# Gated DeltaNet and sliding-window decoder trunk on one core: the mixer's last four gated heads kept in rows, the key halves exchanged by DMA, and other first and last steps of the attention

## The chip, the core and the metric

The kernel runs on one core of a Trainium2 chip. Its time is the device time of one execution in microseconds (us); the time of a version is the median over its runs. The engines are PE (TensorE: matmuls and transposes through the identity), PEld (the weight loads of TensorE, which lie beside the matmuls), DVE (VectorE), ACT (ScalarE), POOL (GpSimd) and SP (SyncE, which here only issues transfers). "L821" is line 821 of the kernel before; where a line of the changed kernel is meant, it says so.

## The reference

The input is x, 512 tokens of 1024 features, in float32. Two layers follow one another:

```python
h = x
h = h + gated_deltanet(rmsnorm(h), w_in, conv_w, ..., w_out)    # layer 0: token mixer
h = h + conv_gated_mlp(rmsnorm(h), w_up, conv_w, conv_b, w_down)
k, v = shared_kv(h, kv_norm_w, w_kv)                            # 4 key and value heads of 64
h = h + sliding_window_sink_attention(rmsnorm(h), k, v, w_q, ..., w_o)   # 16 query heads, window 128
h = h + conv_gated_mlp(rmsnorm(h), ...)
return rmsnorm(h, final_norm_w)
```

Two pieces matter here. The mixer has 16 value heads of 128; at its end each head's output o is normalised and gated, and all heads are projected:

```python
o = rmsnorm(o, out_norm_w) * jax.nn.silu(z)
return o.reshape(bsz, t, GDN_V_DIM) @ w_out
```

The attention has four query heads to a key head: p = softmax over 256 keys and a sink of (q k / 8 + bias), masked to the window; the output p v goes through w_o.

## The kernel before

**Numbers as pairs.** A float32 matrix product is made of three matmuls for each 128 rows of depth: both factors are split into a high part that the matmul takes exactly and the rest (hi and lo), and `mm3` (L158) issues hi by hi (L162), hi by lo (L163) and lo by hi (L164). `split` (L167) makes such a pair of a row of 128 x 512: a cast on ACT (L168) gives hi, a subtraction on DVE (L169) gives lo. Weights come in stages of 1024 x 256 (`load_stage`, L120, two buffers) and are split by `cast` (a cast on ACT, L132, and a subtraction on DVE, L133) into the three buffers each of `whi` and `wlo`.

**Buffers.** Activations lie in rows of 128 x 512 float32, each under a name (`va`, `us`, `p6s`, `dt`, `sz`, `zl`) with a few buffers that go round. A name gives its next buffer out when the last reader of that buffer is done. PSUM has eight banks: three called d, two g, two s, one p.

**End of the mixer.** The table ORDER and the priorities SHIFT set the order of the mixer's jobs: projections, the recurrent `scan` (L609) over four chunks, the gate. `gate_proj` (L684) projects the gate z of a head and writes silu(z) to DRAM (`zd`, L689); `scan` writes o to DRAM (`od`, L666). `gate(h)` (L692) loads o of head h into `dt` (L696) and z into `va` (L697), scales o by its norm on ACT (four instructions of 128 x 128, L700), transposes it on PE into a g bank (L703), multiplies with z on DVE in place (L704) and writes the row to DRAM (`yd`, L705). The last four heads (12 to 15) come after the last chunk of the scan; for them `va` has two buffers. The out-projection then loads each head's row from `yd` (L801) into the rows called "u" (`sz`, `sz`, `zl`), splits it, and multiplies by w_out (`mm3`, the weights from `a_w_out`). Beside it x itself is loaded (L818), transposed on PE into g banks (L821) and copied to the residual rows by ACT (L822); the loads for the last two of its eight parts use buffers that the first two must have left.

**Start of the attention** (`attention`, L1140). Keys and values are projected from the normalised residual. Each of the two key rows holds two key heads of 64. Scores take 64 partitions of queries against 64 partitions of keys, so each key head is needed in both halves of the partitions: L1164 to L1167 cast and subtract every half row twice, into its own half (`near`) and into the other (`far`), eight casts of 64 x 512 on ACT and eight subtractions on DVE. Values are transposed on PE (L1171) and copied by ACT. Then the queries are projected pair by pair (`query`, matmuls L1181, L1183, L1185), and each of the 16 half pairs goes through `scores` (L1224, with a reduction on DVE, L1232, an exponential on ACT, L1249, and a scaling on DVE, L1253), `turn_back` (transposes of the probabilities, L1260) and `values` (L1276). On PE this stretch is in an order that is written out: a generator `dense` gives the matmuls of the later queries and of the first five depth steps of three output tiles one by one, and `take` puts 11 or 12 of them after each half pair.

**End of the attention.** After the last half pair come `values(14)`, the rest of the generator, `turn_back(15)`, depth steps 5 and 6 of the three open output tiles (`late_outputs`), `values(15)`, depth step 7 tile by tile with the addition to the residual on DVE (L1311), and the other five output tiles.

Of the kernel before, what the change touches and what calls it, by code (L numbers as in the profile page):

```python
# [12 lines left out]
ALU = mybir.AluOpType  # L13
# [28 lines left out]
def kernel(  # L42
# [164 lines left out]
    def columns(parts, n, s, q=SP, tag="acc"):  # L207
# [6 lines left out]
        ps = bank("g")  # L214
# [476 lines left out]

    def gate(h):  # L692
        ot, y = (row("ol"), row("zl")) if h < 12 else (row("dt"), row("va"))
# [11 lines left out]
        SP.dma_start(yd[h], y[:])  # L705
# [434 lines left out]
    def attention(h):  # L1140
        toep = rb[:]

        keys = [wide("G") for g in range(4)]
        kxh, kxl = normed(h, NKV)
        for kv in range(2):
# [10 lines left out]
            for i, ps in enumerate(products):  # L1156
                f = r2("va")
                V.tensor_tensor(f[:], ps[:], rs[:], op=ALU.mult)
                if kv == 0:
                    for j in range(2):  # L1160
                        g = 2 * i + j
                        near, far = [slice(64 * u, 64 * u + 64) for u in (j, 1 - j)]
                        src, hi = f[near, :], keys[g][near, 0, :]
                        S.copy(hi, src)  # L1164
                        S.copy(keys[g][far, 0, :], src)
                        V.tensor_tensor(keys[g][near, 1, :], src, hi.bitcast(F32), op=ALU.subtract)
                        V.tensor_tensor(keys[g][far, 1, :], src, hi.bitcast(F32), op=ALU.subtract)  # L1167
                else:
                    pt = bank("g")
                    for c in range(NC):  # L1170
                        PE.transpose(pt[:, c * P : (c + 1) * P], f[:, c * P : (c + 1) * P], ident[:])  # L1171
# [6 lines left out]

        def one_by_one(ps, w, k, xh, xl, first, last):
            hi, lo = w  # L1180
            PE.matmul(ps, hi[:, k, :], xh, start=first, stop=False)  # L1181
# [28 lines left out]
        def scores(u):  # L1210
            p, n0 = u // 2, 2 * (u % 2)
            (qh, ql), b3 = queries[p], bias[p]
            kh, kl = [keys[p // 2][:, i, :] for i in range(2)]
# [4 lines left out]
            for n in (n0, n0 + 1):  # L1218
# [3 lines left out]
                for i, (q, k) in enumerate(((qh, kh), (qh, kl), (ql, kh))):  # L1222
                    for j, hs in enumerate(half):
                        PE.matmul(sc[j][:, at], q[hs, ns], k[hs, k0 : k0 + W], start=i == 0, stop=i == 2)  # L1224
# [82 lines left out]
        def late_outputs(opened, k):  # L1307
            for m, (ps, w) in enumerate(opened):
                yield from one_by_one(ps[:], w, k, ah[k], al[k], False, k == KD - 1)
# [99 lines left out]
```

## Time and profile before

| | |
|---|---|
| median of 3 runs | 1426.94 us (1426.77 to 1426.95) |
| the profiled execution's own time | 1428.72 us |
| its span, from first to last instruction | 1426.9 us |
| mean granted TensorE clock | 0.998 |
| PE busy | 1389.5 us, 97% of the span |
| DVE, ACT, POOL busy | 1113.8, 753.8 and 13.0 us |
| moved by DMA | 152.85 MB, 107 GB/s on average |

The profile is a trace of one execution. A row of a timeline has the start in us from the span's start, the length in us, the engine, the line, the operation, what it writes and reads, a count where several were joined, and in brackets how long the engine had been idle and what ended that. A row of the waits has the engine, what waited, who released it, and the time that was waited. In the windows a row has the stretch, its length, then the busy time and the count of PE, PEld, DVE, ACT and POOL, the granted clock of PE as a share of full speed, the busy share of the DMA engines and GB/s. Matmuls overlap: a row's length is longer than the pace at which they follow one another, so stretches are priced by the distance between starts.

### The profile page before, as it was taken

What the parts mean: (1) busy time and instruction counts of PE and PEld (TensorE: products, weight loads), DVE (VectorE), ACT (ScalarE), POOL (GpSimd) and SP (SyncE); (2) the same over time, 40 slices, a digit from 0 to 9 for tenths busy, and PEclk for the clock granted to TensorE, in tenths of its full rate; (3) what the DMA queues carried; (4) which work ended last, traced back from release to release, by engine and by line L of the source; (5) the groups of instructions that cost most, each with busy time, mean ns of one, the idle gap of its engine ahead of it and who ended that gap; (6) DMA issues with size and microseconds to landing.
All of it is one profiled execution on the core that took longest, in us unless ns stands there. A gap on an engine that the chain in (4) does not pass through costs nothing.

```text
span 1426.9 us, 21762 instructions
## 1 busy us (share of the span) xinstructions
PE 1389.5 (97%) x8362; PEld 1165.5 (82%) x8362; DVE 1113.8 (78%) x2078; ACT 753.8 (53%) x1475; POOL 13.0 (1%) x37
## 2 busy tenths in 40 slices
PE   7999999999998999999999999999999999999997
PEld 5777878878876888888988889778788888988897
DVE  4996887969854447889878889878568888878996
ACT  7764566666546434444334446667544544344443
POOL 1000000000000000000000000000000000000000
PEclk9999999999999999999999999999999999999999
DMA  5324254264466324221443223122132322332222
GB/s 159 103 63 142 79 175 122 73 187 127 141 204 213 118 64 140 90 89 45 133 148 117 75 77 110 55 93 75 38 122 78 111 81 68 125 112 88 96 75 74
DMA packets 163131, 152.85 MB, mean 107 GB/s; under 512 B 24212, under 2 KB 150741, under 8 KB 163029
## 3 DMA queue, kind: packets, MB, share of 16 engines
q1 hardware_dynamic: 160770, 151.27, 33.0%
q8 instruction: 66, 1.08, 0.3%
q10 hardware_dynamic: 2259, 0.20, 0.1%
q14 instruction: 36, 0.29, 0.1%
HBM read 134.65 MB, written 16.80 MB: 106 GB/s over the span
## 4 chain that ended last, share of the span: by engine, by line
PE 82%; DVE 8%; DMA 6%; ACT 2%; issue 1%; DVEq 0%; SPq 0%; ACTq 0%
PE d L162 19%; PE d L163 19%; PE d L164 19%; DVE wlo L133 2%; PE s L617 1%; PE d L1030 1%; PE d L1185 1%; PE d L1028 1%; PE d L1183 1%; PE d L1181 1%; PE d L1029 1%; PE g L1260 1%; PE s L1030 1%; PE p L1276 1%; PE s L657 1%
## 5 line engine op out<-in xcount | busy, mean ns | idle before, releaser
L162 PE MATMUL d<-xh,whi 128*128 128x512 f32 x1128 | 445.1, 396 | 0.2
L163 PE MATMUL d<-xl,whi 128*128 128x512 f32 x1128 | 444.0, 395 | 0.0
L164 PE MATMUL d<-xh,wlo 128*128 128x512 f32 x1128 | 443.2, 395 | 0.7 <-DVE wlo L133 0.4
L132 ACT CAST whi<-stage 128x1024 fp32r<-128x1024 f32 (+2 forms) x234 | 227.3, 975 | 229.2 <-PE d L163 146.8
L133 DVE TENSOR_TENSOR wlo<-stage,whi 128x1024 fp32r<-128x1024 f32 (+2 forms) x234 | 263.5, 1129 | 66.7 <-ACT whi L132 66.2
L164 PEld LDWEIGHTS d<-xh,wlo 128*128 128x128 f32 x1128 | 211.6, 188 | 45.6 <-DVE wlo L133 1.1
L162 PEld LDWEIGHTS d<-xh,whi 128*128 128x128 f32 x1128 | 211.7, 188 | 44.1 <-ACT xh L172 0.5
L163 PEld LDWEIGHTS d<-xl,whi 128*128 128x128 f32 x1128 | 211.7, 188 | 42.9 <-issue 0.5
L260 DVE SCALAR_TENSOR_TENSOR acc<-d,cwc,acc 128x511 f32<-128x511 f32 (+2 forms) x96 | 70.7, 738 | 12.2 <-ACT acc L257 11.6
L911 ACT ACTIVATE dt<-dt 128x512 f32<-128x512 f32 x44 | 27.8, 632 | 80.1 <-DVE dt L894 80.1
L889 DVE TENSOR_TENSOR sz<-d,p6s 128x512 f32<-128x512 f32 x58 | 40.0, 689 | 36.9 <-PE d L164 35.0
L894 DVE SCALAR_TENSOR_TENSOR va<-sz,fcw,va 128x511 f32<-128x511 f32 (+1 forms) x58 | 43.4, 748 | 1.7 <-ACT va L892 0.9
L894 DVE SCALAR_TENSOR_TENSOR dt<-sz,fcw,dt 128x511 f32<-128x511 f32 (+1 forms) x58 | 43.4, 748 | 0.9
L546 DVE TENSOR_TENSOR sT<-sT,p6s 64x31 f32<-64x31 f32 (+15 forms) x124 | 40.8, 329 | 2.2 <-DVE p6s L540 0.3
L540 DVE TENSOR_TENSOR p6s<-sN,sT 64x31 f32<-64x31 f32 (+15 forms) x124 | 40.5, 327 | 2.4 <-DMA sN<-nd 0.4
L1249 ACT ACTIVATE dt<-dt,sm 128x256 f32<-128x256 f32 (+1 forms) x64 | 30.1, 471 | 19.2 <-DVE sm L1232 19.1
L132 ACT CAST whi<-st 128x768 fp32r<-128x768 f32 (+1 forms) x30 | 23.7, 792 | 30.1 <-PE p L1029 5.8
L889 DVE TENSOR_TENSOR zl<-d,p6s 128x512 f32<-128x512 f32 x30 | 20.7, 689 | 24.0 <-PE d L164 23.7
L665 ACT ACTIVATE rq<-o 128x128 f32<-128x128 f32 x64 | 19.0, 298 | 28.6 <-DVE o L660 16.0
L913 DVE TENSOR_TENSOR va<-dt,va 128x512 f32<-128x512 f32 x44 | 30.4, 691 | 1.2
L133 DVE TENSOR_TENSOR wlo<-st,whi 128x768 fp32r<-128x768 f32 (+1 forms) x30 | 26.9, 903 | 2.2 <-ACT whi L132 2.2
L892 ACT ACTIVATE dt<-sz,normc,fcw 128x512 f32<-128x512 f32 x29 | 23.6, 814 | 7.2 <-DVE sz L889 7.2
(770 smaller groups left out, 2866.7 us busy)
## 6 DMA issues: line engine op xcount, KB each, us to landing
stage<-in_ffn_w_up_dram SPq DMA_DIRECT2D x44, 1024.0 KB, 4.9
stage<-in_a_w_in_dram SPq DMA_DIRECT2D x23, 1024.0 KB, 5.1
stage<-in_ffn_w_down_dram SPq DMA_DIRECT2D x16, 768.0 KB, 6.1
stage<-in_a_w_out_dram SPq DMA_DIRECT2D x8, 1024.0 KB, 4.9
st<-in_ffn_w_down_dram SPq DMA_DIRECT2D x8, 768.0 KB
zd<-sz SPq DMA_DIRECT2D x16, 256.0 KB, 2.0
od<-o SPq DMA_DIRECT2D x16, 256.0 KB, 3.7
stage<-in_b_w_q_dram SPq DMA_DIRECT2D x4, 1024.0 KB
```

The source lines that it names most:

```text
L132: S.copy(hi[:, :kt, :m], src)
L133: V.tensor_tensor(lo[:, :kt, :m], src, hi[:, :kt, :m].bitcast(F32), op=ALU.subtract)
L162: PE.matmul(ps, hi[:, k, :m], xh[k], start=first and k == 0, stop=False)
L163: PE.matmul(ps, hi[:, k, :m], xl[k][:], start=False, stop=False)
L164: done.append(PE.matmul(ps, lo[:, k, :m], xh[k], start=False, stop=last and k == kt - 1))
L260: V.scalar_tensor_tensor(acc[:, d:], ps[:, : T - d], col, acc[:, d:], op0=ALU.mult, op1=ALU.add)
L540: V.tensor_tensor(tv, N[:, s, s + 1 : 32].unsqueeze(2).to_broadcast([64, n, m]), Tm[:, s : s + 1, 0:m].to_broadcast([64, n, m]), op=ALU.mult,)
L546: V.tensor_tensor(Tm[:, s + 1 : 32, 0:m], Tm[:, s + 1 : 32, 0:m], tv, op=ALU.subtract)
L889: V.tensor_tensor(u[:], ps[:], rs[:], op=ALU.mult)
L894: V.scalar_tensor_tensor(acc[:, d:], u[:, : T - d], tap(2 - d, t), acc[:, d:], op0=ALU.mult, op1=ALU.add)
L913: V.tensor_tensor(b[:], a[:], b[:], op=ALU.mult)
L1249: S.activation(ej, ej, AF.Exp, bias=ngm[:, i : i + 1], scale=-1.0, accum_out=den[:, i : i + 1])
```

## The change

Six edits, in three places of the kernel; line numbers here are those of the changed kernel.

- **Gate.** Heads 12 to 15 take their gated row in `va`, `va`, `us` and `p6s`, and keep it there; the write to `yd` and the load back are left out for them, and the projection splits straight from these rows.
- **Keys.** One cast and one subtraction of 128 x 512 split a key row for two heads at once; the halves are exchanged into a second pair by DMA, four transfers on SP's queue (L1174), and `scores` takes the head from whichever pair has it in the right half.
- **Table.** A one-column exponential of ACT stands ahead (L1182).
- **Values' transposes** may not be issued ahead of the fourth hi-by-hi matmul of the first query.
- **First half pairs.** Eight of the twelve dense matmuls after the second half pair stand ahead of `turn_back(0)` instead of behind it.
- **Last half pair.** The generator is drained first, nine of the late matmuls follow, then `turn_back(15)`, `values(14)`, five more, `values(15)`, the last four; depth step 7 goes through the three tiles hi by hi, lo by hi and hi by lo, and the three additions come with the last of these.

```diff
     def gate(h):
-        ot, y = (row("ol"), row("zl")) if h < 12 else (row("dt"), row("va"))
+        ot = row("ol" if h < 12 else "dt")
+        y = row("zl") if h < 12 else row(("va", "va", "us", "p6s")[h - 12])
...
-        SP.dma_start(yd[h], y[:])
+        if h < 12:
+            SP.dma_start(yd[h], y[:])
+        else:
+            gated[h] = y
...
-            yr = r2("u")
-            SP.dma_start(yr[:], yd[2 * h2 + j])
+            if h2 < 6:
+                yr = r2("u")
+                SP.dma_start(yr[:], yd[2 * h2 + j])
+            else:
+                yr = gated[2 * h2 + j]
             split(yr[:], a[:, j, :], b[:, j, :])
...
                 if kv == 0:
-                    for j in range(2):
-                        g = 2 * i + j
-                        near, far = [slice(64 * u, 64 * u + 64) for u in (j, 1 - j)]
-                        src, hi = f[near, :], keys[g][near, 0, :]
-                        S.copy(hi, src)
-                        S.copy(keys[g][far, 0, :], src)
-                        V.tensor_tensor(keys[g][near, 1, :], src, hi.bitcast(F32), op=ALU.subtract)
-                        V.tensor_tensor(keys[g][far, 1, :], src, hi.bitcast(F32), op=ALU.subtract)
+                    near, far = keys[i]
+                    split(f[:], near[:, 0, :], near[:, 1, :])
+                    for a, b in ((slice(0, 64), slice(64, 128)), (slice(64, 128), slice(0, 64))):
+                        SP.dma_start(far[a, :, :].bitcast(F32), near[b, :, :].bitcast(F32))
...
+        S.activation(warm[:], rs[:, 0:1], AF.Exp, scale=0.0)
...
+        for t in turned_values:
+            behind(t, issued[3])
...
+                if u == 1:
+                    take(stream, 8)
                 if u > 0:
                     turn_back(u - 1)
-                take(stream, 12 if u < 12 else 11)
-            values(14)
+                take(stream, 4 if u == 1 else 12 if u < 12 else 11)
             for _ in stream:
                 pass
+            rest = late_outputs(opened, range(begun, KD - 1))
+            take(rest, 9)
             turn_back(15)
-            for k in range(begun, KD - 1):
-                for _ in late_outputs(opened, k):
-                    pass
+            values(14)
+            take(rest, 5)
             values(15)
-            for _ in late_outputs(opened, KD - 1):
+            for _ in rest:
                 pass
+            for i in range(3):
+                for m, (ps, w) in enumerate(opened):
+                    PE.matmul(ps[:], w[i % 2][:, KD - 1, :], (ah, ah, al)[i][-1], start=False, stop=i == 2)
+                    if i == 2:
+                        V.tensor_tensor(hT[m], hT[m], ps[:], op=ALU.add)
```

A new argument `place` of `columns` has a default that is the old value and isn't used. What the three places look like in the order of the instructions:

SP's queue at the end of the mixer. `stage` is a weight stage, `f` the rows for x. Before:

```order
L801 DMA sz_4534<-yd 128x512
L122 DMA stage_4755<-in_a_w_out_dram 128x8x256
L705 DMA yd<-va_4325 128x512
L705 DMA yd<-va_4438 128x512
L697 DMA va_4453<-zd 128x512
L801 DMA sz_4544<-yd 128x512
L697 DMA va_4468<-zd 128x512
L801 DMA sz_4548<-yd 128x512
L705 DMA yd<-va_4453 128x512
L818 DMA f_4575<-in_x_dram 128x4x128
L705 DMA yd<-va_4468 128x512
L801 DMA zl_4554<-yd 128x512
```

The same place now, and ahead of it the loads of z for heads 15 and 14:

```order
L689 DMA zd<-sz_4433 128x512
L122 DMA stage_4741<-in_a_w_out_dram 128x8x256
L700 DMA p6s_4465<-zd 128x512
L666 DMA od<-o_4198 128x512
...
L700 DMA us_4451<-zd 128x512
L666 DMA od<-o_4278 128x512
...
L808 DMA zl_4534<-yd 128x512
L122 DMA stage_4743<-in_a_w_out_dram 128x8x256
L827 DMA f_4563<-in_x_dram 128x4x128
L827 DMA f_4564<-in_x_dram 128x4x128
```

The writes of four gated rows, the four loads back and the two loads of z that stood between them are gone from here; the loads of z for heads 14 and 15 are now further up, among the writes of the scan's chunks, and the loads of x follow the weight stage directly.

PE at `turn_back(0)`. `s` are the scores, `g` the banks of the transposes, `d` the dense matmuls. Before:

```order
L1224 MATMUL s_8787<-kT_8384,S_8691 128x256
L1224 MATMUL s_8788<-kT_8384,S_8691 128x256
L1260 MATMUL g_8820<-ident_81,dt_8736 128x128 x2
L1260 MATMUL g_8825<-ident_81,dt_8743 128x128 x4
L1181 MATMUL d_8770<-xh_8639,whi_8771 128x512
```

Now:

```order
L1236 MATMUL s_8768<-kT_8372,S_8672 128x256
L1236 MATMUL s_8769<-qT_8373,S_8672 128x256
L1192 MATMUL d_8751<-xh_8619,whi_8752 128x512
L1194 MATMUL d_8751<-xl_8620,whi_8752 128x512
L1196 MATMUL d_8751<-xh_8619,wlo_8753 128x512
L1192 MATMUL d_8751<-xh_8623,whi_8752 128x512
L1194 MATMUL d_8751<-xl_8624,whi_8752 128x512
L1196 MATMUL d_8751<-xh_8623,wlo_8753 128x512
L1192 MATMUL d_8751<-xh_8627,whi_8752 128x512
L1194 MATMUL d_8751<-xl_8628,whi_8752 128x512
L1272 MATMUL g_8809<-ident_81,dt_8717 128x128 x2
L1272 MATMUL g_8814<-ident_81,dt_8724 128x128 x4
```

Eight dense matmuls have come between the second scores and the transposes, and the two heads' scores read the keys from two tiles, `kT` and `qT`.

PE at the end of the attention, where `p` is the bank of the last values and the three banks d are the open output tiles. Before, from `values(15)` on:

```order
L1276 MATMUL p_9873<-acc_9893,Vp 64x128 x4
L1181 MATMUL d_9646<-at_9846,whi_9647 128x512
L1183 MATMUL d_9646<-at_9847,whi_9647 128x512
L1185 MATMUL d_9646<-at_9846,wlo_9648 128x512
L1181 MATMUL d_9721<-at_9846,whi_9722 128x512
L1183 MATMUL d_9721<-at_9847,whi_9722 128x512
L1185 MATMUL d_9721<-at_9846,wlo_9723 128x512
L1181 MATMUL d_9797<-at_9846,whi_9798 128x512
L1183 MATMUL d_9797<-at_9847,whi_9798 128x512
L1185 MATMUL d_9797<-at_9846,wlo_9799 128x512
L162 MATMUL d_9936<-sy_8964,whi_9937 128x512
```

Now, from the last of the four matmuls that stand behind `values(15)`:

```order
L1196 MATMUL d_9778<-at_9827,wlo_9780 128x512
L1365 MATMUL d_9627<-at_9827,whi_9628 128x512
L1365 MATMUL d_9702<-at_9827,whi_9703 128x512
L1365 MATMUL d_9778<-at_9827,whi_9779 128x512
L1365 MATMUL d_9627<-at_9827,wlo_9629 128x512
L1365 MATMUL d_9702<-at_9827,wlo_9704 128x512
L1365 MATMUL d_9778<-at_9827,wlo_9780 128x512
L1365 MATMUL d_9627<-at_9828,whi_9628 128x512
L1365 MATMUL d_9702<-at_9828,whi_9703 128x512
L1365 MATMUL d_9778<-at_9828,whi_9779 128x512
L162 MATMUL d_9917<-sy_8945,whi_9918 128x512
L163 MATMUL d_9917<-sy_8946,whi_9918 128x512
```

The last matmul that reads the high weights of the first tile was the second of nine and is the seventh now; the next output tile needs that buffer.

More of the change, by code (lines that the diff above doesn't have):

```diff
@@ L1176, in attention @@
         ah, al = [], []
+        issued = []
         def one_by_one(ps, w, k, xh, xl, first, last):
             hi, lo = w
-            PE.matmul(ps, hi[:, k, :], xh, start=first, stop=False)
+            issued.append(PE.matmul(ps, hi[:, k, :], xh, start=first, stop=False))
             yield
```

27 lines of the change are left out of this document (15 added, 12 removed).

## Prediction

> **What bounds the kernel now.** I read the page first: the span, the busy times, the chain that ended last.
>
> ```profile
> span 1426.9 us, 21762 instructions
> PE 1389.5 (97%) x8362; PEld 1165.5 (82%) x8362; DVE 1113.8 (78%) x2078; ACT 753.8 (53%) x1475; POOL 13.0 (1%) x37
> PE 82%; DVE 8%; DMA 6%; ACT 2%; issue 1%; DVEq 0%; SPq 0%; ACTq 0%
> ```
>
> PE is busy for all but 37.4 us of the span, and it holds 82% of the chain. The change takes next to no matmul away, so whatever it brings must come out of PE's idle time or its clock at the three places it touches. So I read PE's waits next (time in total, how often, the longest):
>
> ```profile
> PE g L821 <- DVE va L704: 3.5, 1, 3.5
> PE g L1260 <- DVE dt L1253: 2.2, 1, 2.2
> PE p L1276 <- DVE at L169: 0.7, 1, 0.7
> PE d L1181 <- ACT at L168: 0.7, 1, 0.7
> PE d L1183 <- DVE at L169: 0.2, 1, 0.2
> ```
>
> Each is a single wait, and each lies at one of the three places: the transposes of x at the end of the mixer, `turn_back(0)`, and the end of the attention. The longest has a second price, which the windows show (PE busy, granted clock in the eighth place):
>
> ```profile
> 453.50:457.00 3.50, 0.03 (x1) 0.06 (x2) 0.75 (x1) 0.34 (x1) 0.00 (x0) 1.00 0.69 217
> 457.00:460.00 3.00, 3.00 (x13) 2.52 (x14) 1.79 (x3) 1.48 (x3) 0.00 (x0) 0.59 0.76 259
> ```
>
> PE stands for 3.5 us, and then runs with a clock of 0.59 for 3 us: another 0.41 x 3.0 = 1.2 us.
>
> **Part 1, the gated rows.** Why PE waited there:
>
> ```profile
> SPq L697 <- DMA yd<-va: 6.2, 1, 6.2
> 453.42 0.32 SPq L697 DMA_DIRECT2D va<-zd  x1
> 456.07 0.75 DVE L704 SCALAR_TENSOR_TENSOR va<-g,onwc,va 128x512 f32<-128x512 f32 x1 [5.55 <-DMA va<-zd]
> 457.63 0.38 SPq L818 DMA_DIRECT2D f<-in_x_dram  x1
> f<-in_x_dram SPq DMA_DIRECT2D x5, 256.0 KB, 4.1
> 442.49 4.79 ACT L700 ACTIVATE dt<-dt,fc 128x128 f32<-128x128 f32 x16 [0.57 <-DMA dt<-od]
> 447.19 0.60 ACT L168 CAST at<-sz 128x512 fp32r<-128x512 f32 x1
> 447.85 0.73 PE L162 MATMUL d<-at,whi 128*128 128x512 f32 x2
> 462.00 1.12 PE L821 MATMUL g<-ident,st 128*128 128x128 f32 x8
> 462.88 0.47 PE L162 MATMUL d<-ktok,whi 128*128 128x512 f32 x1
> 468.77 0.39 PE L162 MATMUL d<-sy,whi 128*128 128x512 f32 x1
> 491.89 0.39 PE L162 MATMUL d<-kT,whi 128*128 128x512 f32 x1
> ```
>
> Heads 14 and 15 need `va` again, so SP waited 6.2 us for the writes of heads 12 and 13 to land, issued the load of z at 453.42, and DVE could gate head 14 only at 456.07, after 5.55 us idle. The g banks of the last two heads stayed taken until then, and the transposes of x need them. With rows of their own all four heads find z loaded; all sixteen scalings on ACT are done at 442.49 + 4.79 = 447.28, and the four gates should be done near 448.6.
>
> What the stretch is worth I take from work against time. From 468.77 to 491.89 lie 102 dense matmuls and nothing else: 23.12 / 102 = 0.2267 us each. The eight transposes at 462.00 take until 462.88: 0.11 each. From 447.85 to 468.77 PE executes 49 dense matmuls and 32 transposes: 49 x 0.2267 + 32 x 0.11 = 14.6 us of work in 20.9 us. So 6.3 us are lost, of which the wait and its clock explain 4.7. The order now has the same set of work for PE in this stretch. What stays: ACT has four casts of 0.6 us for the rows, a weight cast and the copies of x in front of PE's banks, for which I leave 0.8 us. Parts 6 and 7 of x are loaded into the buffers of parts 0 and 1. Before, that load (457.63) followed those transposes by 0.7 us; now they run near 448 to 449, the loads go out by 449.6 and land 4.1 us later, at 453.7, about 2 us before PE comes to them. **Gain 5.5 us**, at most 6.3; at least 3.5, the bare wait.
>
> The loads of z for heads 15 and 14 moved up SP's queue, and a load into `p6s` now waits for its z to have been written:
>
> ```profile
> 420.06 0.32 SPq L689 DMA_DIRECT2D zd<-sz  x1
> zd<-sz SPq DMA_DIRECT2D x16, 256.0 KB, 2.0
> 422.45 0.32 SPq L666 DMA_DIRECT2D od<-o  x1
> ```
>
> The write goes out at 420.06 and lands 2.0 us later, at 422.1. Behind the wait stands the write of o, which itself goes out at 422.45, so it costs 0. Were the landing to take the 4.1 us of a load of x, SP would come 1.7 us late to that write and to the loads of gated rows behind it, which PE needs later; I allow 0.8 us for that end. The load into `us` waits for the last readers of `us`, the same matmuls for which the write of o behind it waits: 0.
>
> **Part 2, start of the attention.**
>
> ```profile
> 908.90 0.59 ACT L863 COPY p6s<-g 128x512 f32<-128x512 f32 x1 [3.21 <-PE g L861]
> 910.25 0.62 ACT L1164 CAST kT<-va 64x512 fp32r<-64x512 f32 x1 [0.76 <-DVE va L1158]
> 914.73 0.62 ACT L1165 CAST nt<-va 64x512 fp32r<-64x512 f32 x1
> 915.37 2.56 ACT L172 ACTIVATE xh<-h,normc 128x512 fp32r<-128x512 f32 x4
> 916.54 1.29 DVE L1158 TENSOR_TENSOR va<-d,p6s 128x512 f32<-128x512 f32 x2
> 916.15 0.50 PE L1181 MATMUL d<-xh,whi 128*128 128x512 f32 x1
> 917.28 1.25 PE L1171 MATMUL g<-ident,va 128*128 128x128 f32 x8 [0.63 <-DVE va L1158]
> 918.54 0.50 PE L1183 MATMUL d<-xl,whi 128*128 128x512 f32 x1
> 929.55 0.44 PE L1224 MATMUL s<-kT,rq 64*128 64x128 f32 x4
> 931.10 1.28 ACT L1249 ACT_TABLE_LOAD   x1
> 932.73 0.40 ACT L1249 ACTIVATE dt<-dt,sm 128x128 f32<-128x128 f32 x1 [0.35 <-DVE sm L1232]
> 937.00 1.09 PE L1260 MATMUL g<-ident,dt 128*128 128x128 f32 x6 [2.19 <-DVE dt L1253]
> ```
>
> *Casts.* Eight casts from 910.25 to 915.35 become two of a full row, 0.6 us each: the key casts end near 912, and the eight queries' `xh` (0.64 each) are through by 917.1 instead of following 915.37. DVE loses six subtractions and can form the value rows (916.54, two in 1.29) about 0.5 us earlier, by 917.4. From 916.15 to 918.54 PE did one dense matmul and eight transposes, 0.23 + 0.88 = 1.11 us of work in 2.39: 1.3 us lost to late operands. Now ten dense matmuls stand ahead of the transposes (2.3 us), which puts them at 918.2, with 0.8 us to spare: **1.3 us gained**.
>
> *Table.* The load (1.28 us) goes from 931.10 to the gap of ACT behind 909.49. Where it was, the exponential behind it still waited 0.35 us for DVE, so it hid: 0 gained. Where it is, it ends at 910.8, pushes the key casts by 0.5 us at most, and the 0.8 us above cover it. If the cover is gone, 0.5 us are lost. The Trainium skill (ScalarE: Activation LUTs, What ACT_TABLE_LOAD costs) counts a drain of some 1.4 us with such a load, 2.7 us together; by that the casts would slip by 1.9 us and the sum be 1.1 us less. The row shows 1.28 us and no such stand behind it, so I go by the row.
>
> *`turn_back(0)`.* PE arrived at 934.81 and waited 2.19. Scores to transposes took 929.55 to 937.00, 7.45 us; with scores 1.3 earlier the transposes are ready at 935.70. PE arrives at 933.51, does eight dense matmuls (1.81) until 935.32, and waits 0.4. Gain against before: 937.00 - 935.70 + 1.81 = 3.1 for casts and `turn_back` together; with ACT and DVE relieved a little more. **Part 2: 3.2 us**, bounds 2 and 4.
>
> *Exchange.* Four transfers of 256 KB leave SP near 913, when both subtractions are done, and must land by 928.2. A row of 256 KB lands in 4.1 us; my value is 5 to 6 us for the four, hidden; the other end is four one behind the other, 16.4 us, until 929.5, 1.3 us late. The second pair and the weight loads queued behind them are not due by then.
>
> **Part 3, end of the attention.**
>
> ```profile
> 1028.02 0.39 PE L162 MATMUL d<-sy,whi 128*128 128x512 f32 x1
> 1026.62 2.94 ACT L132 CAST whi<-stage 128x1024 fp32r<-128x1024 f32 x3 [1.31 <-PE d L1183]
> ```
>
> The three waits at L1276, L1181 and L1183 (0.7 + 0.7 + 0.2 = 1.6 us, some 2 with the restarts) are covered now: five dense matmuls (1.1 us) stand between `values(14)` and `values(15)`, four behind it (0.9) against a cast of 0.6. But the weight cast for the next output tile began when the first tile's high weights were read for the last time (1026.62), with seven matmuls (1.6 us) ahead of PE to hide 0.98 us of it; now two are left (0.45), and the casts for the following two tiles come as closely. I count 0.7 us for the first and 0.6 for the others: 1.3 lost. **Net 0.7 us**, bounds -0.8 (the lost time doubled) and 2.
>
> **The sum.** 5.5 + 3.2 + 0.7 = 9.4 us. The profiled execution took 1428.72 us (span 1426.9), so this one would take 1419.3; the median is 1.78 us below it, and 1426.94 - 9.4 = 1417.5. The reordered loads in the channel mixer behind this, four buffers further round, I cost at 0: PE has no wait there that this touches, and a slip of one load would be under 1 us.
>
> **The rivals.**
>
> *x comes late.* The gap at 453.5 is exchanged for one at parts 6 and 7 of x, since their loads hang on the transposes of parts 0 and 1 and on a landing time that was taken at less traffic. For it: the DMA share is 0.69 to 0.76 there. Against it: the loads and writes that made that traffic are gone. If landing takes 6 us and more, part 1 is worth 3: 1420.0. Chance 0.16.
>
> *The exchange is serial.* By rows 16.4 us, scores 1.3 us late: 1418.8. Chance 0.08. The Trainium skill (DMA: Bandwidth & Descriptors, Rules for kernel authors) speaks against such transfers: of two to disjoint partition halves it says "Don't bother — they serialize". No row of before has such a pair.
>
> *The exchange is the new bound.* It is the way to slower. The scores of the first pair can't begin before it lands, and everything on PE stands behind them. A stand of 3.5 us cost another 1.2 by the clock, so all gains are gone when PE stands from 928.2 on for 8.2 us. It decides at a landing near 936.4, 23 us after issue; slower by more than 0.2% (2.9 us, about what a measurement of this kernel can tell from no change) from 939.3 on. At 940 it would be 1426.94 - 9.4 + 11.8 + 1.2 = 1430.5. Four times 4.1 us is far from it. Chance 0.02.
>
> *The end gives nothing.* The three banks and weight buffers come free together and the casts stand one behind the other: part 3 at -0.8, 1419.0. Chance 0.14.
>
> *The edit does not take.* `turn_back(0)` still waits as long as before, since the chain through ACT and DVE grew by as much: part 2 at 1.3, 1419.4. Chance 0.05.
>
> **How the numbers follow.** The forecast has the rest, 0.55. The range: the upper bounds 6.3 + 4 + 2 = 12.3 give 1414.6; below, two rivals at once (x late, the end nothing, 3 + 3.2 - 0.8 = 5.4) 1421.5, of which I take 1421.2. Under 1424.1 is faster by more than 0.2%: all cases but the slower one and a pile of mishaps: 0.95; within 0.2% 0.03; slower 0.02.
>
> **What would show it.** In the changed profile: no wait of PE on DVE's gate and no clock below 0.9 from 450 to 465, the tile's matmul of 468.77 near 463.3; the first scores near 922.7 (928.2 less the 5.5 us of part 1), `turn_back(0)` with a wait under 0.5; the exchange landed by then; at the end no wait on `at`, but one on ACT's `whi` cast behind the last nine matmuls. The prediction is wrong if the first place keeps more than 2 us of waits, if scores wait for a DMA, or if other places of PE's list grow.

## The result and the profile after

Five runs of the changed kernel took 1419.19 us in the median (1417.68 to 1422.22), five of the kernel before 1426.95 (1426.77 to 1429.68): 7.8 us less, a ratio of 0.994 with a 95% interval of 0.9922 to 0.9957. The profiled executions are further apart: 1428.72 before, 1419.19 after, 9.5 us. The forecast was 1417.5 in a range of 1414.6 to 1421.2.

The page of the changed kernel, its span, busy times and chain:

```profile
span 1417.3 us, 21741 instructions
PE 1385.0 (98%) x8362; PEld 1164.1 (82%) x8362; DVE 1108.7 (78%) x2072; ACT 749.5 (53%) x1470; POOL 13.1 (1%) x37
PE 85%; DVE 7%; DMA 4%; ACT 3%; issue 1%; SPq 0%; DVEq 0%; ACTq 0%
```

PE executes the same 8362 matmuls and its idle time is 5 us shorter; its busy time is 4.5 us shorter too. 1.7 us of that are the slow clock of before behind the transposes of x, which is gone; where the rest lies I have not taken apart. The slow stretch of before, at half clock from end to end:

```profile
457.55:460.97 3.42, 3.42 (x14) 2.76 (x13) 1.90 (x3) 1.79 (x3) 0.00 (x0) 0.50 0.76 265
```

The new waits of PE at the places of the change:

```profile
PE d L162 <- ACT kT L168: 1.3, 1, 1.3
PE d L162 <- ACT whi L132: 1.1, 3, 0.7
PE p L1288 <- DVE sy L169: 0.8, 1, 0.8
```

The waits of 3.5 us (transposes of x) and of 2.2 us (`turn_back(0)`) are gone, and so are those on the splits of the last values. The first new one is a cast of a gated row late in the mixer, the second the weight casts behind the last open output tiles, the third a later `values`. One more wait of 0.9 us is new in code that was not touched (L414, at 205 us); it stands in some of the traces below too. The mixer's end in windows, and single rows there (PE, SP):

```profile
450.00:455.00 5.00, 5.00 (x31) 4.08 (x29) 3.89 (x6) 4.42 (x9) 0.00 (x0) 1.00 0.39 110
455.00:460.00 5.00, 5.00 (x27) 4.20 (x27) 2.58 (x3) 3.69 (x6) 0.00 (x0) 1.00 0.00 0
```

```profile
440.64 0.50 PE L162 MATMUL d<-kT,whi 128*128 128x512 f32 x1 [1.33 <-ACT kT L168]
448.74 1.49 SPq L827 DMA_DIRECT2D f<-in_x_dram  x2
455.04 1.15 PE L830 MATMUL g<-ident,f 128*128 128x128 f32 x8
463.30 0.39 PE L162 MATMUL d<-sy,whi 128*128 128x512 f32 x1
```

PE is busy all through, at full clock. The last two parts of x are loaded from 448.74 on and PE transposes them at 455.04 without a wait. The matmul that started at 468.77 starts at 463.30.

The start of the attention (SP, DVE, PE):

```profile
907.11 1.16 SPq L1174 DMA_DIRECT2D qT<-kT  x2
910.84 0.69 DVE L1169 TENSOR_TENSOR va<-d,p6s 128x512 f32<-128x512 f32 x1
912.91 1.03 PE L1179 MATMUL g<-ident,va 128*128 128x128 f32 x8
922.50 0.32 PE L1236 MATMUL s<-kT,rq 64*128 64x128 f32 x1
929.59 0.82 PE L1272 MATMUL g<-ident,dt 128*128 128x128 f32 x6
```

The second value row is formed by 911.5, PE transposes at 912.91; the first scores start at 922.50 and `turn_back(0)` at 929.59, none of them with a wait. The end (PE, ACT):

```profile
1016.84 0.84 PE L1365 MATMUL d<-at,whi 128*128 128x512 f32 x3
1017.26 2.95 ACT L132 CAST whi<-stage 128x1024 fp32r<-128x1024 f32 x3 [2.14 <-PE d L1365]
1018.36 0.50 PE L162 MATMUL d<-sy,whi 128*128 128x512 f32 x1 [0.68 <-ACT whi L132]
```

The last four of the late matmuls and the nine of depth step 7 follow `values(15)` without a wait; then the weight cast can only begin at 1017.26, and PE stands for 0.68 us, and 0.22 twice for the two casts behind.

**Four stretches.** Total times carry everything that varies in 1400 us, so I compare the traces by stretches between instructions that every kernel has. On DVE these are the start of the row with the last four updates of the scan's state (L646; 426.90 before, 427.03 after), the first convolution input of the first channel mixer (L889 before, 539.24; L898 after, 533.78), its last, the scaling of the first and of the last query (L1200, L1211), and the last addition of the output tiles (L1350, L1371). In us:

| kernel | A: scan to channel mixer | B: channel mixer to first query | C: first to last query | D: last query to last output tile |
|---|---|---|---|---|
| before | 112.3 | 87.2 | 71.7 | 60.2 |
| after | 106.8 | 85.7 | 70.2 | 59.5 |
| e1_gate | 106.8 | 87.2 | 73.2 | 60.2 |
| e2_start | 110.2 | 85.3 | 70.2 | 60.2 |
| e3_end | 108.8 | 86.9 | 73.2 | 59.5 |
| e4_keys | 111.0 | 85.7 | 72.8 | 60.1 |
| e5_loop | 110.9 | 87.4 | 69.8 | 60.2 |
| e6_no_table | 106.0 | 85.5 | 69.8 | 59.5 |
| e7_rows_trip | 109.9 | 85.2 | 70.2 | 59.5 |
| e8_four_times | 107.1 | 85.1 | 72.6 | 59.5 |
| e9_end_mixed | 106.4 | 85.4 | 70.2 | 58.8 |
| e11_best | 106.0 | 85.2 | 70.2 | 58.8 |
| e12_four | 110.1 | 87.4 | 70.8 | 60.2 |

Between A and B lies the channel mixer, the same in all: 297.7 to 298.9. Before against after: 5.6 in A, 1.6 in B, 1.5 in C, 0.7 in D, 9.3 together. The spans differ by 9.6; the rest, some 0.4 behind D less 0.1 ahead of A, lies in code that both have alike.

### The profile page after: what moved, and what is told of

Same layout as the page of the kernel before. It is cut to its first block, busy times and chain, and to the rows that moved or that the text cites. A ratio compares the mean times of both kernels' runs of the same rounds, so it can differ in the third digit from the quotient of the medians.

```text
span 1417.3 us, 21741 instructions
## 1 busy us (share of the span) xinstructions
PE 1385.0 (98%) x8362; PEld 1164.1 (82%) x8362; DVE 1108.7 (78%) x2072; ACT 749.5 (53%) x1470; POOL 13.1 (1%) x37
## 4 chain that ended last, share of the span: by engine, by line
PE 85%; DVE 7%; DMA 4%; ACT 3%; issue 1%; SPq 0%; DVEq 0%; ACTq 0%
PE d L162 19%; PE d L164 19%; PE d L163 19%; DVE wlo L133 2%; PE s L617 1%; PE d L1192 1%; PE d L1196 1%; PE d L1194 1%; PE d L1039 1%; PE d L1037 1%; PE d L1038 1%; PE s L1039 1%; PE s L657 1%; PE p L1288 1%; DMA ol<-od 1%
## 5 line engine op out<-in xcount | busy, mean ns | idle before, releaser
L260 DVE SCALAR_TENSOR_TENSOR acc<-d,cwc,acc 128x511 f32<-128x511 f32 (+2 forms) x96 | 70.8, 739 | 12.2 <-ACT acc L257 11.5
L898 DVE TENSOR_TENSOR sz<-d,p6s 128x512 f32<-128x512 f32 x59 | 40.6, 688 | 43.8 <-PE d L164 41.6
L898 DVE TENSOR_TENSOR zl<-d,p6s 128x512 f32<-128x512 f32 x29 | 19.9, 688 | 17.8 <-PE d L164 17.8
```

What stands on the lines that cost most here:

```text
L260: V.scalar_tensor_tensor(acc[:, d:], ps[:, : T - d], col, acc[:, d:], op0=ALU.mult, op1=ALU.add)
L898: V.tensor_tensor(u[:], ps[:], rs[:], op=ALU.mult)
```

## The experiments

### One place alone

Three kernels carry one of the three places each. The edits are hunks of the diff above: for `e1_gate` those of `gate` and of the projection,

```diff
-        ot, y = (row("ol"), row("zl")) if h < 12 else (row("dt"), row("va"))
+        ot = row("ol" if h < 12 else "dt")
+        y = row("zl") if h < 12 else row(("va", "va", "us", "p6s")[h - 12])
```

for `e2_start` the keys, the table, the values' transposes and the loop,

```diff
+                    near, far = keys[i]
+                    split(f[:], near[:, 0, :], near[:, 1, :])
...
+        S.activation(warm[:], rs[:, 0:1], AF.Exp, scale=0.0)
...
+                if u == 1:
+                    take(stream, 8)
```

and for `e3_end` the order behind the loop.

```diff
+            rest = late_outputs(opened, range(begun, KD - 1))
+            take(rest, 9)
             turn_back(15)
...
+            for i in range(3):
+                for m, (ps, w) in enumerate(opened):
+                    PE.matmul(ps[:], w[i % 2][:, KD - 1, :], (ah, ah, al)[i][-1], start=False, stop=i == 2)
```

> The kernel before with the gated rows alone (heads 12 to 15 in rows of their own, no trip through DRAM). Theory: the 3.5 us wait of PE at the transposes of x and the slow clock behind it go, and the first channel mixer starts 5.5 us earlier by the trace; a time of about 1421.4 us. Rival (the three places are not independent, the gain here is partly lost again in a later wait): the first channel mixer starts 5.5 us earlier, but the end of the span only 3 to 4 us.

Measured: 1426.76 us (1424.06 to 1428.09) against 1430.26 of the kernel before beside it, ratio 0.9977 (0.9967 to 0.9986): some 3.3 us less, so the theory's 1421.4 was missed. A is 106.8, as in the changed kernel, and the channel mixer starts 5.6 us earlier than in the trace of before. The end of the span, though, is only 2.6 us earlier, nearer to the rival's numbers. But its reason, a later wait that takes the gain, isn't what happened. 1.0 us went in the channel mixer, whose instructions are the same, 1.5 us in C, which `e3_end`, without the gated rows, shows as well, and 0.6 us behind D, where nothing differs either. For C the windows behind `turn_back(0)`'s wait say why; first before, then `e1_gate`:

```profile
937.00:940.00 3.00, 2.98 (x16) 2.44 (x17) 1.73 (x9) 1.87 (x7) 0.00 (x0) 1.00 0.20 59
```

```profile
932.33 1.09 PE L1269 MATMUL g<-ident,dt 128*128 128x128 f32 x6 [2.19 <-DVE dt L1262]
933.70:937.11 3.41, 3.41 (x9) 2.63 (x8) 1.48 (x6) 0.93 (x4) 0.00 (x0) 0.50 0.29 82
```

The same wait of 2.19 us left the clock at 1.00 in the profiled execution of before, and took it to 0.50 for 3.41 us here: 0.50 x 3.41 = 1.7 us.

> The kernel before with the start of the attention alone (keys by two splits and four transfers, the exponential's table ahead, the values' transposes later, eight dense matmuls ahead of the first turn_back). Theory: 1.6 us by the end of the first query, 3.0 us by the last queries, and as much at the end; about 1423.9 us. Rival (the gain in the changed kernel hung on the earlier parts): under 2 us at the last query.

Measured: 1425.26 (1423.64 to 1425.92), ratio 0.9965 (0.9951 to 0.9978). B 85.3 and C 70.2, each within 0.4 of the changed kernel's: 1.9 and 1.5 us less than before. The rival (under 2 us by the last query) falls: it is 3.4.

> The kernel before with the end of the attention alone. Theory: the waits on the last values and their splits (1.6 us with the restarts some 2) go, waits on the weight casts of the next three output tiles (about 1.1 us) come, net 0.7 us: 1426.2 us, not to be told from no change by the time, but by the trace. Rival: the gain and the loss belong to different causes, and alone the edit loses 0.5 us or more.

Measured: 1427.38 (1425.75 to 1431.96), ratio 0.9984 (0.9973 to 0.9995). D 59.5 against 60.2, 0.69 us, with the same three waits on the weight casts as in the changed kernel (1.1 us together). The gain and the loss come together, as the theory has it, and the rival (a loss of 0.5 us or more) falls. The total is 0.16% lower (0.05 to 0.27%), 2.3 us, more than these 0.7; the rest lies outside D, in code that the edit leaves alone, and there single executions differ by as much, as the next lines show for A.

Left without the gated rows, `e2_start` and `e3_end` have A at 110.2 and 108.8, not at 112.3. So the mixer's end of before varies from one execution to the next, and the profile had caught a long one. The wait at the transposes of x in six executions of that unchanged code: 3.5 us in before, 2.9 in `e5_loop`, 2.4 in `e4_keys`, 2.0 in `e2_start`, 1.1 in `e3_end` and `e12_four`. The rows of `e5_loop` and of `e2_start`:

```profile
456.15 1.09 PE L821 MATMUL g<-ident,f 128*128 128x128 f32 x4 [2.88 <-DVE va L704]
456.00:459.00 3.00, 2.85 (x10) 2.39 (x11) 1.92 (x4) 1.48 (x3) 0.00 (x0) 0.50 0.62 213
```

```profile
455.61 0.63 PE L821 MATMUL g<-ident,f 128*128 128x128 f32 x4 [2.00 <-DVE va L704]
456.00:459.00 3.00, 2.78 (x19) 2.02 (x17) 2.02 (x3) 2.14 (x4) 0.00 (x0) 1.00 0.70 228
```

The wait of 2.88 us cost a clock of 0.50 as well, as those of 3.54 us in before and of 2.4 in `e4_keys` did; that of 2.00 us cost only itself. In `e2_start` and `e12_four` PE waited another 0.8 and 1.1 us there for x itself. The wait goes largely with the landing of the writes of the gated rows, for which SP stood 6.2 us in before and in `e4_keys`, 6.0 in `e5_loop`, 5.2 in `e2_start`, and 4.4 in `e3_end` and `e12_four`:

```profile
SPq L697 <- DMA yd<-va: 4.4, 1, 4.4
```

(this row is of `e12_four`, with a wait of 1.1 us on PE). Over the six executions that keep the trip through DRAM as it was, A is 110.6 in the mean (108.8 to 112.3); over five with the edit it is 106.6 (106.0 to 107.1). The gated rows are worth 4.0 us on average, and 5.6 against the execution that was profiled.

### Rows of their own, but the trip stays

```diff
-        if h < 12:
-            SP.dma_start(yd[h], y[:])
-        else:
-            gated[h] = y
+        SP.dma_start(yd[h], y[:])
...
-            if h2 < 6:
-                yr = r2("u")
-                SP.dma_start(yr[:], yd[2 * h2 + j])
-            else:
-                yr = gated[2 * h2 + j]
+            yr = r2("u")
+            SP.dma_start(yr[:], yd[2 * h2 + j])
```

> The changed kernel, but the four gated rows, each in its own row, are still written to DRAM and loaded back for the projection. It parts the two things that the edit does. Theory (both count: the reuse of the rows held the gates, the trip holds the projection): the transposes of x have no long wait, but the split rows of heads 12 to 15 come 3 to 6 us later, and the first channel mixer starts 2 to 3.5 us later than in the changed kernel. Rival (the reuse of the two rows was all): within 0.5 us of the changed kernel.

Measured: 1422.17 us in one run; A 109.9, 3.3 us above the mean of the kernels with the edit. The transposes of x don't wait, and instead PE waits for a row that came back (PE's rows of `e7_rows_trip`):

```profile
457.80 0.50 PE L162 MATMUL d<-ktok,whi 128*128 128x512 f32 x1 [1.43 <-ACT ktok L168]
458.52 0.50 PE L163 MATMUL d<-ktok,whi 128*128 128x512 f32 x1 [0.23 <-DVE ktok L169]
```

The first channel mixer starts at 536.51, 2.7 us later than in the changed kernel (533.78), as the theory has it, and the rival (the reuse of two rows was all) falls. Most of the 4.0 us comes from leaving the trip out. What the rows alone bring, 0.7 us by this one trace (110.6 - 109.9), can't be told from nothing, as A went from 108.8 to 112.3 in kernels that have neither.

### The start of the attention in parts

`e4_keys` has only the hunks on the keys; `e5_loop` only the loop, with eight, and `e12_four` with four matmuls ahead of `turn_back(0)`; `e6_no_table` is the changed kernel without the early exponential.

```diff
+                if u == 1:
+                    take(stream, 4)
                 if u > 0:
                     turn_back(u - 1)
-                take(stream, 12 if u < 12 else 11)
+                take(stream, 8 if u == 1 else 12 if u < 12 else 11)
```

```diff
-        S.activation(warm[:], rs[:, 0:1], AF.Exp, scale=0.0)
```

> The kernel before with the keys alone: two splits and four transfers, all else at the start of the attention as before (the order of PE puts the first value transposes one dense matmul earlier than before). Theory: ACT and DVE get free some 3 us sooner, but the value rows are not formed before the values' projection is done, so the transposes make PE wait still; the first scores come 0.5 to 1 us earlier than before, and PE still waits about 2 us at the first turn_back. Rival (the casts were the whole of it): the first scores 1.5 us earlier.

Measured: 1427.16 in one run. B is 85.7, 1.5 us less than the 87.2 of before, and the first scores start 1.6 us earlier, counted from the end of the channel mixer: the rival. PE still waits 2.2 us at the first `turn_back`, as the theory has it. The value rows in `e4_keys` on DVE, and the transposes on PE:

```profile
910.89 0.69 DVE L1158 TENSOR_TENSOR va<-d,p6s 128x512 f32<-128x512 f32 x1
915.26 0.69 DVE L1158 TENSOR_TENSOR va<-d,p6s 128x512 f32<-128x512 f32 x1
```

```profile
915.06 0.60 PE L1167 MATMUL g<-ident,va 128*128 128x128 f32 x4
916.00 0.66 PE L1167 MATMUL g<-ident,va 128*128 128x128 f32 x4
```

DVE, free of the half subtractions, forms the first value row long before PE comes, and the second as soon as its part of the values' projection is done, while PE does two matmuls between the two sets of transposes. What made PE wait before was DVE's queue, not the end of the values' projection; the fixed place of the transposes adds little: B is 85.3 in the mean of the seven kernels that have both, and 85.7 in the changed kernel itself.

> The kernel before with eight dense matmuls ahead of the first turn_back instead of behind it, nothing else. Theory: eight matmuls (1.8 us) fill the wait of 2.2 us, 0.4 us of it stays; later half pairs may give some back, since their dense work is the same: 1.5 to 1.8 us earlier at the last queries. Rival (a wait of the same size comes at the next turn_back, whose cover has moved): under 0.5 us.

Measured: 1426.03 in one run. C is 69.8: 1.9 us less than before, 3.0 to 3.4 less than the executions with the slow clock. PE's wait at `turn_back(0)` is 0.2 us, and no later one takes its place: the rival falls, and the theory's 1.5 to 1.8 us were a little too few.

> The kernel before with four instead of eight dense matmuls put ahead of the first turn_back. PE's wait there falls from 2.2 to about 1.3 us. Theory (behind a wait of 2.2 us the clock falls in some executions, as in three of four traces of kernels that keep it, where from the first to the last query's end it was 72.8 to 73.2 us instead of 71.7; a wait of 1.3 us has only its own price): no clock below 0.9 behind it, and 70.7 us from the first to the last query's end. Rival (the clock falls behind any wait here): 71.9 to 72.3 us and a clock of 0.5 to 0.75 for 3 us.

Measured: 1428.63 in one run. C is 70.79, as the theory gave it. The wait and the clock behind it:

```profile
937.87 1.09 PE L1260 MATMUL g<-ident,dt 128*128 128x128 f32 x6 [1.07 <-DVE dt L1253]
937.90:940.90 3.00, 2.97 (x16) 2.20 (x18) 1.73 (x10) 2.06 (x8) 0.00 (x0) 1.00 0.23 62
```

A wait of 1.07 us left the clock at 1.00 in this execution, against the rival. It is one draw, but the wait of 1.1 us at the transposes of x, in this trace and in that of `e3_end`, left it at 1.00 too.

> The changed kernel without the one-column exponential, so that the table is loaded where the first exponential of the scores is, as before. Theory: the load of 1.28 us hides behind the reduction on DVE as it did before; the first turn_back waits no longer, the time differs by less than 0.3 us. Rival (with ACT and DVE relieved the load is the last to end there): the first turn_back 0.5 to 1.3 us later.

Measured: 1420.52 in one run. C is 69.8, 0.4 us shorter than with the early table. The load is hidden where it was before:

```profile
925.91 1.28 ACT L1260 ACT_TABLE_LOAD   x1
927.53 0.40 ACT L1260 ACTIVATE dt<-dt,sm 128x128 f32<-128x128 f32 x1 [0.34 <-DVE sm L1243]
```

With the load moved, ACT and DVE take the work of the first half pairs in another order: `turn_back(0)` doesn't wait at all (0.2 us without the move), but a `values` waits 0.8 us on DVE later, the third row of the waits after. That wait of 0.8 us stands in all five traces with the early table whose scores don't wait (C is 70.2 in each: the changed kernel, `e2_start`, `e7_rows_trip`, `e9_end_mixed`, `e11_best`). It is in neither trace that has the eight matmuls and the table where it was (`e6_no_table` and `e5_loop`, C 69.8). So the move costs 0.4 us.

### The exchange, four times

```diff
-                    for a, b in ((slice(0, 64), slice(64, 128)), (slice(64, 128), slice(0, 64))):
+                    for a, b in (4 if i == 0 else 1) * ((slice(0, 64), slice(64, 128)), (slice(64, 128), slice(0, 64))):
```

> The changed kernel with the exchange of the first two key heads' halves made four times, each pair of transfers waiting until the one before it has landed; the result is the same. The distance of the pairs on SP's queue is what one pair takes to land. Theory: both halves move at once, some 3 to 4 us to a pair, the fourth lands by 922 (in the changed kernel's trace the first went out at 907.1 and the first scores began at 922.5), PE waits 0 to 1 us there and the time stays within 1 us. Rival (the halves go one after the other, 4.1 us each): 8 us to a pair, the fourth lands near 940, the scores wait some 16 us, and the time is near 1435 us.

Measured: 1423.84 in one run. SP's rows of the four pairs, and PE's at the first scores:

```profile
908.78 1.16 SPq L1174 DMA_DIRECT2D qT<-kT  x2
911.96 1.69 SPq L1174 DMA_DIRECT2D qT<-kT  x2
915.57 1.63 SPq L1174 DMA_DIRECT2D qT<-kT  x2
919.72 1.62 SPq L1174 DMA_DIRECT2D qT<-kT  x2
```

```profile
926.52 0.32 PE L1236 MATMUL s<-qT,rq 64*128 64x128 f32 x1 [1.97 <-DMA qT<-kT]
927.17:930.58 3.41, 3.41 (x12) 2.60 (x9) 2.56 (x12) 1.96 (x9) 0.00 (x0) 0.50 0.11 35
```

Pairs follow at 3.2, 3.6 and 4.2 us; the last, with two weight loads of 1 MB issued around it, landed 6.8 us after its issue. Nearer to the theory than to 8 us a pair, which falls. But the fourth landed at 926.5 where I had 922, and behind the wait of 1.97 us the clock was 0.50 for 3.4 us. The time is 4.7 us above the median of the changed kernel, not within 1; C has 2.4 of them, the rest lies in code that both have alike. By these pairs one exchange is done 3 to 4 us after its issue. In the changed kernel the first goes out at 907.1, DMA goes quiet at 912.8 (a busy share of 0.75 until there, 0.01 in the 2 us behind it), and the first scores start 9.7 us after that. The Trainium skill (DMA: Bandwidth & Descriptors, Rules for kernel authors) says of two transfers to disjoint partition halves that they serialize, since they share the same DMA engines; 3.2 us for both together, where a single transfer of 256 KB takes 2.0 (`zd`) to 4.1 us (`f`) in the profile of before, doesn't show it as a doubling, and at this place it would be hidden anyway.

### Two edits on top

```diff
-            for i in range(3):
-                for m, (ps, w) in enumerate(opened):
-                    PE.matmul(ps[:], w[i % 2][:, KD - 1, :], (ah, ah, al)[i][-1], start=False, stop=i == 2)
-                    if i == 2:
-                        V.tensor_tensor(hT[m], hT[m], ps[:], op=ALU.add)
+            for m, i in ((0, 0), (0, 1), (1, 0), (0, 2), (1, 1), (1, 2), (2, 0), (2, 1), (2, 2)):
+                ps, w = opened[m]
+                PE.matmul(ps[:], w[i % 2][:, KD - 1, :], (ah, ah, al)[i][-1], start=False, stop=i == 2)
+                if i == 2:
+                    V.tensor_tensor(hT[m], hT[m], ps[:], op=ALU.add)
```

> The changed kernel with the last nine matmuls of the three open output tiles in another order: the first tile is done after four of them, the second after six, the third after nine. Theory: the casts of the next weights then begin after the fourth matmul instead of after the seventh; the first cast's wait of PE (0.68 us) goes, the two later ones (0.22 each) grow to some 0.5, and the next channel mixer starts 0.7 to 0.9 us earlier than in the changed kernel. Rival (what bounds that place is not the release of the weight buffers but the three additions on DVE or the landing of the weights): no difference.

Measured: 1418.29 (1417.29 to 1418.45, four runs), ratio to before 0.9917 (0.99 to 0.9933). D is 58.8, 0.68 us less than in the changed kernel. The rows of `e9_end_mixed`, ACT and PE:

```profile
1016.54 2.94 ACT L132 CAST whi<-stage 128x1024 fp32r<-128x1024 f32 x3 [1.45 <-PE d L1365]
```

```profile
1017.65 0.50 PE L162 MATMUL d<-sy,whi 128*128 128x512 f32 x1
1018.59 0.50 PE L162 MATMUL d<-sy,whi 128*128 128x512 f32 x1 [0.21 <-ACT whi L132]
```

The casts begin 0.7 us earlier and all that follows does too; the wait of 0.68 is gone. The two others stay at 0.2 and don't grow to 0.5, as the casts come one behind the other in both kernels. The rival (no difference) falls.

`e11_best` has this order and one word more:

```diff
-        y = row("zl") if h < 12 else row(("va", "va", "us", "p6s")[h - 12])
+        y = row("zl") if h < 12 else row(("va", "va", "acc", "p6s")[h - 12])
```

> The changed kernel with two edits: the last nine matmuls in the mixed order (the first tile done after four of them), and the gated row of head 14 in a row called acc instead of us, so that SP's queue is not held by the last readers of us (1.7 us in the changed kernel) with loads of gated rows behind it. Theory: 0.7 us at the end, and the new wait of PE on a cast of a gated row (0.9 to 1.5 us in four traces) becomes shorter by some 1 us: about 1.5 us less than the changed kernel. Rival (that wait hangs on the landing of the load or on the order in which PE takes the rows, not on SP): only the 0.7 us at the end.

Measured: 1418.71 (1417.04 to 1419.98, six runs), ratio 0.9917 (0.9902 to 0.9933). D 58.8 again. SP's wait of the changed kernel for the last readers of `us`,

```profile
SPq L700 <- PE s L657: 1.7, 1, 1.7
```

is gone, and so is PE's wait on the cast of a gated row, 0.9 to 1.6 us in the other five traces. But the one didn't make the other. The rows of the changed kernel (SP, SP, ACT), then those of `e11_best`:

```profile
434.11 0.32 SPq L700 DMA_DIRECT2D us<-zd  x1
435.45 0.32 SPq L808 DMA_DIRECT2D sz<-yd  x1
439.97 0.62 ACT L168 CAST kT<-sz 128x512 fp32r<-128x512 f32 x1 [1.79 <-DMA sz<-yd]
```

```profile
434.90 0.32 SPq L808 DMA_DIRECT2D sz<-yd  x1
437.54 0.62 ACT L168 CAST kT<-sz 128x512 fp32r<-128x512 f32 x1
```

The cast for which PE waits has the row of the first load behind the load of z. That load goes out only 0.1 us earlier against the last update of the scan, 7.5 us behind it instead of 7.6: without the load into `us`, SP stands 2.4 us there for the next write of o. What differs is the landing, 4.5 us after the issue in the changed kernel and 4.0 to 4.9 in the other kernels with `us`, 2.6 in `e11_best`. So it is nearer to the rival, which named the landing. In the kernels with `us` the load of z, 256 KB, goes out just ahead of that row, and with `acc` 28 us sooner; that the two held each other up on the DMA engines is likely, but one trace without it doesn't show it. A is 106.0 against 106.6 in the mean of those five, whose spread is 1.0: a gain of half a microsecond or none. In total times neither kernel can be told from the changed one; by D both are 0.7 us faster.

## Why the prediction was right

**The sum** of 9.4 us, with terms of 5.5, 3.2 and 0.7, became 9.35 in the traces: 5.6, 3.05 (1.6 + 1.5) and 0.7. The profiled executions differ by 9.5. The median moved less, by 7.8, and the forecast for it was 1.7 us too low. The long wait in the profiled execution of before pushes that way, its unspoilt clock at `turn_back(0)` the other way; what made the difference isn't shown. Beside later kernels the kernel before took 1429.4 to 1430.5 in the median, so the gain in the median itself is known to some 3 us only.

**Part 1** was right in its mechanism: the wait and the slow clock are gone, and the matmul forecast near 463.3 starts at 463.30. Its size is right against that one execution, and in part by luck. The clock was priced at 1.2 us, since the window of 0.59 began ahead of the slow stretch; it was 0.50 for 3.4 us, 1.7 us, so that wait and clock explain 5.2 of the 6.3 us lost. And what the prediction took as a property of the kernel, the wait of 3.5 us and its clock, is a draw: 1.1 to 3.5 us in six executions, with the slow clock in three of them. On average the term is 4.0. The step on SP's queue held: the load into `us` cost SP next to nothing, as costed, and the wait on the landing of z (422.23 for the load, 422.64 for the write of o) cost 0.2 us where 0.8 had been allowed. What the step left out is the landing of the gated row that is loaded behind it, for which ACT and then PE waited, 0.9 to 1.6 us on PE. The prediction named the growth of other waits on PE as a sign against it, and this wait and the 0.8 us of a later `values` are such, small against what went.

**Part 2.** The casts gave 1.6 us instead of 1.3. The cover that I named, ten matmuls ahead of the transposes, isn't what did it: the keys alone bring 1.5. The eight matmuls ahead of `turn_back(0)` were put at some 1.8 and the whole at 3.1; C gained 1.5 against the profiled execution, and 2.6 to 3.0 against those with the old loop whose clock fell behind the wait, which I had not counted since the profile of before showed 1.00 there. The table was costed at 0, and is worth -0.4. The rows behind the load (ACT of the changed kernel):

```profile
904.30 1.28 ACT L1182 ACT_TABLE_LOAD   x1
905.60 0.20 ACT L1182 ACTIVATE warm<-p6s 128x1 f32<-128x1 f32 x1
905.70 0.60 ACT L168 CAST kT<-va 128x512 fp32r<-128x512 f32 x1
```

The exponential starts 0.02 us behind the load and the first key cast 0.1 us after that, some 0.7 us later than its row allowed, and PE's transposes didn't wait for it. So the loss of 1.1 us that the drain on the Trainium skill's page (ScalarE: Activation LUTs, What ACT_TABLE_LOAD costs) would have given isn't there.

**Part 3** came out as computed, 0.7 net, with 1.1 us of waits on weight casts where 1.3 were counted. That the joint release of the weight buffers costs this is shown by the mixed order, which gives 0.68 back.

**The rivals.** x didn't come late. The exchange took 5.7 us, between the forecast 5 to 6, and is hidden by 9.7 us, neither serial to a harmful degree nor the bound; made four times it did become late, by 2.0 us, which shows that the mechanism of the slower case exists and how far off it was. The end gave its 0.7 us in D, and `turn_back(0)` does not wait.

## What to carry to other kernels

A wait that hangs on the landing of a DMA is a random size: one profile shows one draw, and several traces of code that was not touched tell what it is worth; compare stretches between fixed instructions rather than total times when terms are under 0.2%. A short wait of PE costs its length, and behind waits of 1.7 to 3.5 us here the clock fell in some executions and cost up to 1.7 us more, so work that only cuts a wait from 2.2 to 1.1 us can bring most of it. When a buffer is taken for something that is loaded, look who else must leave it, where its load then stands on the queue, and which load stands right behind it: here that one landed 2.6 us behind its issue without the new load ahead of it, and 4.0 to 4.9 with it, though the cause is not shown.

## What was not expected of the hardware

Wherever the clock fell here between the start and the last steps of the kernel, it fell to 0.50 for 3.41 us, which costs 1.7 us at most. It fell behind waits of PE of 3.5 us (before), 2.9 (`e5_loop`), 2.4 (`e4_keys`), 2.2 (`e1_gate`, `e3_end`, `e4_keys`), 2.0 (`e8_four_times`) and, at an untouched place near 45 us (L215), of 1.7 to 1.85 us in four traces. It did not fall behind the 2.2 us of before, the 2.0 of `e2_start`, the waits of 1.1, and 1.7 to 1.85 us at that same place in nine other traces. The shortest wait that cost it, in `e9_end_mixed`:

```profile
44.67 0.50 PE L215 MATMUL g<-ident,f 128*128 128x128 f32 x2 [1.69 <-DVE onwc L217]
45.00:48.42 3.42, 3.42 (x14) 3.05 (x14) 2.25 (x7) 1.75 (x4) 0.00 (x0) 0.50 0.94 296
```

The Trainium skill (TensorE: Matmul & The Clock Gate, What's actually happening) gives a window of some 3.4 us that runs freely. The 3.41 us agree with it, and a window that runs freely fits waits of equal length with and without the loss. The same page (Why this matters for your kernels) asks for gaps of no more than some 3 us; here the clock was lost behind gaps well under that, down to 1.69 us.

What is open: the size of the gain from `acc` in place of `us`, and what makes the landings differ. Why the channel mixer between the stretches takes 297.7 to 298.9 us in kernels that have it unchanged is known in part: PE waits there on one weight cast, 146 us into it, for nothing in before and for 0.6 to 0.7 us in `e1_gate`, `e12_four` and `e11_best`, and that cast waits for its weights to land.
